# Product banks written whole before they are read, y a slot later, and token orders changed, in a fused GLA and S5 decoder block

## The chip, the cores and the metric

The kernel runs on one core of a Trainium2 chip. The metric is the device time of one execution in microseconds (us), and the time given is the median of several runs. Beside these runs stands one execution taken with the hardware profiler; from it come the profile's page and the answers of the trace. The engines are called as in the profile: PE is TensorE (PEld its weight loads), DVE is VectorE, ACT is ScalarE, POOL is GpSimd, SP is the engine that here only issues transfers. L60 means line 60 of the kernel.

## The reference, cut to what matters

One decoder block over 512 tokens of width 1024, all in fp32. 16 meta tokens stand ahead of the 512, so the mixers see 528 tokens.

```
h    = concat(meta, x);  xn = rmsnorm(h);  proj = xn @ w_in
q, k, v, r, a_low, u, z_gla, z_ssm = split(proj)
# GLA, 4 heads, key width 128, value width 256, chunks:
S_t  = diag(alpha_t) S_{t-1} + k_t^T v_t ;  o_t = q_t S_t      (alpha from a_low @ w_gate_up)
y_gla = (rmsnorm(o) * silu(r)) @ w_o_gla
# S5, 64 groups of 16 channels, 64 complex states each:
x_t  = Lbar x_{t-1} + Bbar u_t ;  y_t = Re(C x_t) + D u_t
y_ssm = glu(gelu(y) @ w_glu + b_glu)
mixed = sigmoid(z_gla) * y_gla + sigmoid(z_ssm) * y_ssm
h    = h + rmsnorm(mixed @ w_out)
f    = relu(rmsnorm(h) @ w_ff1)^2 @ w_ff2
out  = (h + rmsnorm(f)) without the meta tokens
```

## The kernel before, in words

**Products.** Every large product is made of three passes on PE. An fp32 operand is split into a rounded part and its remainder: ACT writes the rounded part (`split_hi`, L149), DVE subtracts it from the operand (L162 for weights, `wlo`). PE then adds hi x hi, hi x lo and lo x hi in one bank (`mm3`). A weight tile of 128 columns therefore costs a transfer of 512 KB on SP (`wraw`), one ACT and one DVE instruction, and 24 matmuls of 512 columns, or 48 of 264 columns where meta tokens are needed too. `xh` and `xl` hold the split, normalised input with features on the partitions and the 528 tokens along the columns, meta first.

**Banks.** There are two PSUM pools of four banks: `mm` for the large products, `sm` for small ones. A `sm` bank is taken again for the fifth allocation after it, once the readers of its old content are done. Two accesses of different engines to one bank are kept apart by a wait, also where they touch different halves.

**The mixer stage** is one long list, `dense`, of weight tiles. `slot()` takes the next tile, asks for the weights of the two tiles after it (`AHEAD = 2`, three buffers), and runs its matmuls and their epilogue. Between the slots stands the small work of the S5 scan (eight blocks of eight groups, class `Block`) and of the GLA heads (four, class `Head`; head h belongs to block h). In the order of one block b of the loop over blocks:

- `turns`: the rotation factors E of the block (DVE, ACT); then a slot
- `kernels`: turns MB into M1 on PE, makes the short kernel, issues the eight loads of U on SP; then `outputs` of the head before (products of scores and values and of queries and states, their squares on ACT, a chain of twelve small DVE steps to the row scale `ors`, and the scaled rows `on` on ACT) and `decays` of this head (exponentials from a load of `b2`); then a slot
- `scan`: M1 times U into `vv`, a swap of its halves by two transfers on POOL, rotation (L879), scan over chunks (L882), a second swap on POOL, rotation back (L885, L886), which gives X. On the side it stores the short kernel and issues the eight loads of M3. Then `turn_outputs` of the head before (transposes of `on`, one scaling, a store on POOL each); then a slot
- `turn_values`, a slot, `turn_keys`, a slot
- `scores` and `states` of this head. `states` makes four products, two to a bank; the first is copied out by DVE (L766), the others are added to the decayed state before (L769)
- `output`: y = M3 times U plus M2 times X in one bank, gelu on ACT and DVE, and eight stores on POOL (L903), which put y into phase order (token t of chunk c goes to column t*64 + c, with eight tokens to a chunk).

The order of PE's instructions through this stage is pinned to the order of the program. The order of the other engines' instructions, and of the transfers in each issuing queue, is set by a planner from its own estimates, before the kernel runs; at run time every queue is strictly in order.

**The merge** loads the eight tiles of gelu(y), splits them into `gh` and `gl` (L1008, L1009) while putting the tokens back into their order, and runs the GLU products; it reads the stored gates `zs` and GLA outputs `td`. Then come the output projection by tiles of 128 tokens (with a second load of x), and the feed-forward part, which is dense on PE to the end.

Of the kernel before, what the change touches and what calls it, by code (L numbers as in the profile page):

```python
# [22 lines left out]
HALF = NT // 2  # L23
# [13 lines left out]
T8 = 8  # L37
# [12 lines left out]
def hybrid_block(ctx: ExitStack, tc: tile.TileContext, io, out: bass.AP):  # L50
# [169 lines left out]
    xh, xl = (mk(px, [P, KT, LINE + SEQ], F32R, tag=t)[:, :, LINE - NM :] for t in ("xh", "xl"))  # L220
# [4 lines left out]

    def u_half(w, ut, q):
        ps = bank("mm")
        last = feat_tile(w, xh, xl, q * HALF, (q + 1) * HALF, ps[:, :HALF])
        S.copy(ut[:, :, q * 33 : (q + 1) * 33].rearrange("p s c -> p c s"), ps[:, :HALF].rearrange("p (c s) -> p c s", s=T8))
        return last  # L230
# [13 lines left out]
    xm = mk(pxt, [P, D], tag="xt", bufs=5)  # L244
    nc.scalar.dma_start(grow, io["g_mix_pre"][0].rearrange("(o d) -> o d", o=1))
    nc.scalar.dma_start(xm[:NM], io["meta_tokens"])
    xts = [(xm, NM, 0)]
    for t in range(TT):
        xt = mk(pxt, [P, D], tag="xt", bufs=5)
        loaded = nc.sync.dma_start(xt, io["x"][0, t * P : (t + 1) * P, :])  # L250
        xts.append((xt, P, NM + t * P))
# [13 lines left out]
    V.memset(ss[:, 0:1], 1.0)  # L265
    for i, (xt, n, col) in enumerate(xts):
        sq = mk(pxt, [P, D], tag="xsq", bufs=2)
        squared = S.activation(sq[:n], xt[:n], AF.Square, accum_out=ss[:n, i : i + 1])
        if i == 0:
            continue  # L270
        a = 0 if i == 1 else i
        root(rs[:, a : i + 1], ss[:, a : i + 1], pxt, f"xr{min(i, 2)}")
        for xt, n, col in xts[a : i + 1]:
            j = (col + P - 1) // P
            xn = mk(pxt, [P, D], tag="xn", bufs=2)
            normed = V.scalar_tensor_tensor(xn[:n], xt[:n], rs[:n, j : j + 1], gpre[:n], op0=ALU.mult, op1=ALU.mult)
            with ExitStack() as after:
                if i > 2:
                    after.enter_context(tc.issue_after(fed.ins))
                transpose_tokens(xn[:n], n, xh, xl, col)  # L280
        if i == 2:
# [3 lines left out]
        if i in (2, 3):  # L285
            fed = u_half(uw[i - 2], uts[i - 2], 0)
# [20 lines left out]
    for c in [0] + [NM + P * i for i in range(TT)]:  # L307
        G.memset(mask01[:, c : c + 1], 0.0)
# [10 lines left out]
    def low_rank():  # L319
        for i in range(2):  # L320
            sl = slice(i * HALF, (i + 1) * HALF)
            ps = bank("mm")
            for k in range(KT):
                PE.matmul(ps[:32, :HALF], wa[:, k, :], xh[:, k, sl], start=(k == 0), stop=False, skip_group_check=True)
                PE.matmul(ps[:16, :HALF], wa[:, k, :16], xl[:, k, sl], start=False, stop=(k == KT - 1), skip_group_check=True)
            S.copy(alow[:, sl], ps[:32, :HALF])
# [5 lines left out]
    def gate_up(h):  # L332
        for i in range(2):
            sl = slice(i * HALF, (i + 1) * HALF)
            ps = bank()
            PE.matmul(ps[:, :HALF], wgu[:, h * P : (h + 1) * P], alow[:, sl], start=True, stop=True)
            bg = vecs[:, V_BGATE + h : V_BGATE + h + 1]
            S.activation(ga[:, h, sl], ps[:, :HALF], AF.Abs, bias=bg)
            V.tensor_scalar(mn[:, h, sl], ps[:, :HALF], bg, 0.0, op0=ALU.add, op1=ALU.min)
# [316 lines left out]
    class Head:  # L656
# [10 lines left out]
        def value(self, w):  # L667
            vt = mk(pgb, [P, NT], tag="vt", bufs=2)
            for i in range(2):
                ps = bank("mm")  # L670
                feat_tile(w, xh, xl, i * HALF, (i + 1) * HALF, ps[:, :HALF])
                S.copy(vt[:, i * HALF : (i + 1) * HALF], ps[:, :HALF])
            self.vt.append(vt)

        def turn_values(self):
            self.vtok = mk(pgb, [P, TT, DV], tag="vtok", bufs=2)
            self.vmeta = mk(pgb, [NM, DV], tag="vmeta", bufs=2)
            for j, vt in enumerate(self.vt):
                cc = slice(j * P, (j + 1) * P)
                ps = bank()  # L680
                for t in range(TT):
                    PE.transpose(ps[:, t * P : (t + 1) * P], vt[:, NM + t * P : NM + (t + 1) * P], ident)
                S.copy(self.vtok[:, :, cc], ps.rearrange("p (t c) -> p t c", t=TT))
            ps = bank()
            for j, vt in enumerate(self.vt):
                PE.transpose(ps[:NM, j * P : (j + 1) * P], vt[:, :NM], ident)
            S.copy(self.vmeta, ps[:NM, :DV])

        def decays(self):
            b2 = mk(pgb, [P, NT], tag="b2")  # L690
            nc.sync.dma_start(b2, bd[self.h])
            bm = b2[:, NM:].rearrange("p (c t) -> p c t", t=CH)
            bp = b2[:, NM:].rearrange("p (c t) -> p c t", t=P)
# [7 lines left out]
            V.tensor_sub(dl[:, NM:].rearrange("p (c t) -> p c t", t=P), bp, bp[:, :, P - 1 : P].to_broadcast([P, TT, P]))  # L701
            V.tensor_scalar(dl[:, :NM], b2[:, :NM], b2[:, NM - 1 : NM], None, op0=ALU.subtract)
# [10 lines left out]
            self.qg = ex([P, SEQ], b2[:, NM:], "gq", 1.0 / TAU)  # L713

        def key(self, w):
            kT = mk(pgb, [P, NT], tag="kT")
            for i in range(2):
                ps = bank("mm")
                feat_tile(w, xh, xl, i * HALF, (i + 1) * HALF, ps[:, :HALF])
                S.copy(kT[:, i * HALF : (i + 1) * HALF], ps[:, :HALF])  # L720
            V.tensor_mul(self.kg, kT, self.kg)
            V.tensor_mul(self.kin, kT[:, NM:], self.kin)
            V.tensor_mul(self.kx, kT[:, NM:].rearrange("p (c t) -> p c t", t=P)[:, :, :CH], self.kx)

        def query(self, w):
            qs = DK ** -0.5
            ps = bank("mm")
            feat_tile(w, xh, xl, NM, NT, ps)
# [4 lines left out]
        def turn_keys(self):  # L733
            kg = self.kg
            ps = bank()
            for t in range(TT - 1):
                PE.transpose(ps[:, t * P : (t + 1) * P], kg[:, NM + t * P : NM + (t + 1) * P], ident)
            PE.transpose(ps[:NM, 3 * P : 4 * P], kg[:, :NM], ident)
# [18 lines left out]
        def states(self):  # L757
            self.st = []
            for t in range(TT):
# [445 lines left out]
```

## Time and profile before

| what | value |
|---|---|
| median of 3 runs | 1024.34 us (1023.4 to 1025.26) |
| the profiled execution | 1023.0 us, span 1021.3 us |
| PE busy | 963.2 us (94% of the span) |
| DVE, ACT, POOL busy | 559.1, 380.8, 92.8 us |
| mean granted clock of PE | 0.959 |
| a block of the mixer stage with a head | 59.0 us (207.69 to 266.72) |

The span is the profiled execution without what lies around it. A row of waits reads: the engine and its bank's name, then `<-` the engine, tile and line that released it, then microseconds in total, how many times, and the longest. A row of the timeline has start and duration in microseconds, then the engine, line, operation and tiles; square brackets hold the idle time before the first of the group and its releaser. A row of windows has the stretch, its length, and for each engine its busy time and number of instructions; then comes PE's granted clock (1.00 is full) and the transfers' share. A row of groups gives the busy time and the mean in nanoseconds of one instruction.

### The profile page before, as it was taken

To read this page: it belongs to the slowest core of one execution; us is meant where nothing else is said; L and a number is where in the kernel's file an instruction comes from. 1 tells how busy PE (TensorE), PEld (TensorE's weight loads), DVE (VectorE), ACT (ScalarE), POOL (GpSimd) and SP (SyncE) were. 2 spreads that over 40 slices of the span, in tenths; PEclk is the share of its full clock that TensorE was granted. 3 is DMA by queue.
4 is the path that set the end of the run, shared out by engine and by line. 5 is a ranking of instruction groups with operands and counts; after the bars stand their busy time and mean duration, and the time that the engine had idled before them with its cause. 6 is when DMAs were issued, how large, how long until landed. Compare 5 with 4: busy or idle time off the path is not lost.

```text
span 1021.3 us, 13307 instructions
## 1 busy us (share of the span) xinstructions
PE 963.2 (94%) x5052; PEld 824.0 (81%) x5052; DVE 559.1 (55%) x1003; ACT 380.8 (37%) x614; POOL 92.8 (9%) x189
## 2 busy tenths in 40 slices
PE   5999989989797999899989999999999999999997
PEld 4898969879696888788868887798888888888885
DVE  6779974645647469764445466563333343333335
ACT  6354534534443244222234244443232233233222
POOL 1220101111020112212200000000000000000000
PEclk9999988979698899799999999999999999999998
DMA  6835452425234266475585566123333354323302
GB/s 199 181 118 152 133 142 53 127 55 135 59 72 121 53 170 165 122 188 145 162 268 155 154 189 202 63 83 103 86 101 103 95 192 146 98 88 104 102 23 83
DMA packets 156801, 127.42 MB, mean 125 GB/s; under 512 B 22541, under 2 KB 137297, under 8 KB 156738
## 3 DMA queue, kind: packets, MB, share of 16 engines
q1 hardware_dynamic: 147472, 103.14, 36.2%
q0 software_dynamic: 8224, 20.74, 6.9%
q10 hardware_dynamic: 1042, 2.69, 0.7%
q8 instruction: 40, 0.66, 0.3%
q14 instruction: 23, 0.19, 0.1%
HBM read 103.37 MB, written 18.91 MB: 120 GB/s over the span
## 4 chain that ended last, share of the span: by engine, by line
PE 66%; issue 13%; DVE 10%; DMA 5%; ACT 3%; POOL 2%; DVEq 0%; POOLq 0%; SPq 0%; ACTq 0%
PE mm L60 47%; PE sm L60 18%; DMA vv<-vv 2%; DVE wlo L162 2%; DMA qi<-qd 1%; PE sm L65 1%; DMA wraw<-in_w_out_dram 1%; DVE vv L885 1%; ACT whi L149 1%; DMA wraw<-in_w_in_dram 1%; DMA wraw<-in_w_ff_dram 0%; DVE epb L210 0%; DVE ht L1089 0%; DVE mta L209 0%; DVE vv L886 0%
## 5 line engine op out<-in xcount | busy, mean ns | idle before, releaser
L162 DVE TENSOR_TENSOR wlo<-wraw,whi 128x1024 fp32r<-128x1024 f32 x104 | 126.9, 1220 | 150.3 <-ACT whi L149 143.8
L149 ACT ACTIVATE whi<-wraw 128x1024 fp32r<-128x1024 f32 x104 | 110.0, 1059 | 241.3 <-PE mm L60 223.9
L60 PE MATMUL mm<-xh,whi 128*128 128x264 f32 (+1 forms) x544 | 186.5, 343 | 0.3 <-ACT xh L149 0.3
L60 PE MATMUL mm<-xl,whi 128*128 128x264 f32 (+1 forms) x544 | 182.2, 335 | 0.7 <-DVE xl L187 0.7
L60 PE MATMUL mm<-xh,wlo 128*128 128x264 f32 (+1 forms) x544 | 181.7, 334 | 0.0
L60 PEld LDWEIGHTS mm<-xh,whi 128*128 128x128 f32 x544 | 106.6, 196 | 10.5 <-ACT xh L149 1.0
L60 PEld LDWEIGHTS mm<-xl,whi 128*128 128x128 f32 x544 | 106.4, 196 | 9.8 <-DVE xl L187 1.2
L60 PEld LDWEIGHTS mm<-xh,wlo 128*128 128x128 f32 x544 | 106.0, 195 | 9.2
L60 PE MATMUL mm<-hh,wlo 128*128 128x512 f32 (+1 forms) x280 | 103.9, 371 | 0.0
L60 PE MATMUL mm<-hl,whi 128*128 128x512 f32 (+1 forms) x280 | 103.8, 371 | 0.0
L60 PE MATMUL mm<-hh,whi 128*128 128x512 f32 (+1 forms) x280 | 103.8, 371 | 0.0
L1147 DVE TENSOR_TENSOR fl<-f,fh 128x512 fp32r<-128x512 f32 x32 | 22.2, 693 | 90.7 <-ACT fh L149 90.6
L149 ACT ACTIVATE fh<-f 128x512 fp32r<-128x512 f32 x32 | 20.2, 632 | 108.4 <-PE sm L60 104.7
L60 PEld LDWEIGHTS mm<-hh,whi 128*128 128x128 f32 x280 | 52.8, 188 | 9.1
L60 PEld LDWEIGHTS mm<-hh,wlo 128*128 128x128 f32 x280 | 52.8, 188 | 9.0
L60 PEld LDWEIGHTS mm<-hl,whi 128*128 128x128 f32 x280 | 52.8, 188 | 9.0
L60 PE MATMUL mm<-gh,whi 128*128 128x512 f32 x128 | 50.1, 396 | 3.2 <-ACT gh L149 3.2
L60 PE MATMUL mm<-gl,whi 128*128 128x512 f32 x128 | 50.5, 397 | 1.4 <-DVE gl L1009 1.4
L60 PE MATMUL mm<-gh,wlo 128*128 128x512 f32 x128 | 49.9, 395 | 0.0
L60 PE MATMUL sm<-U,M 128*128 128x65 f32 (+1 forms) x256 | 48.9, 315 | 0.0
L60 PEld LDWEIGHTS sm<-U,M 128*128 128x128 f32 x256 | 44.6, 235 | 1.4
L1143 DVE TENSOR_TENSOR w2l<-wraw,w2h 128x1024 fp32r<-128x1024 f32 x32 | 39.1, 1225 | 10.1 <-ACT w2h L149 10.1
(386 smaller groups left out, 1726.0 us busy)
## 6 DMA issues: line engine op xcount, KB each, us to landing
wraw<-in_w_ff_dram SPq DMA_DIRECT2D x64, 512.0 KB, 3.8
wraw<-in_w_in_dram SPq DMA_DIRECT2D x48, 512.0 KB, 4.3
wraw<-in_w_glu_dram SPq DMA_DIRECT2D x16, 512.0 KB, 4.2
vv<-vv POOLq DMA_DIRECT2D x32, 130.0 KB, 4.2
xt<-in_x_dram SPq DMA_DIRECT2D x8, 512.0 KB, 6.2
M<-kpad SPq DMA_DIRECT2D x64, 64.0 KB, 4.9
wraw<-in_w_o_gla_dram SPq DMA_DIRECT2D x8, 512.0 KB, 4.4
wraw<-in_w_out_dram SPq DMA_DIRECT2D x8, 512.0 KB, 4.3
```

What stands on the lines that cost most here:

```text
L60: ins = nc.tensor.matmul(*args, **kw)
L65: ins = nc.tensor.transpose(*args, **kw)
L149: S.activation(dst, src, AF.Copy, scale=scale)
L162: V.tensor_sub(lo[:, :, :n], raw[:, :, :n], f32(hi)[:, :, :n])
L885: V.tensor_mul(vv, vv, self.E)
L1143: V.tensor_sub(lo, raw, f32(hi))
L1147: V.tensor_sub(fl, f[:, k], f32(fh))
```

## The change

- **Whole banks.** `states` issues both products of a bank before DVE reads either; `outputs` issues all eight products of its two banks before ACT's squares.
- **Order of the blocks' small work.** `output` of block b moves behind `kernels` of block b+1; `outputs` of a head moves behind `scan`, with the exponential `qg` behind it (`query_decay`); `turn_outputs` moves behind `turn_values`. In blocks 6 and 7 one slot of five is left out; one more stands before the last `output`, and the list of tiles has three gates ahead of the r tiles instead of two.
- **Token order of S5.** The order of the columns after the merge stays the phase order of y. The sigmoid gates are written in that order (`by_phase`, `phases`: a read of the bank with a stride of eight columns), the GLA output's product reads its bank so, and the merge's splits become contiguous. Behind the output projection the rows of x and of the result are loaded and stored in pieces of 64 rows with a stride of eight tokens.
- **Meta tokens last.** The columns of `xh` and `xl` are the 512 tokens, then meta; halves of 256 and 272 columns take the place of two of 264. Meta is normalised after the four x tiles, each with a root of its own.
- The tiles `qi` of the merge get four buffers instead of two.

```diff
-HALF = NT // 2
+HALVES = ((0, 256), (256, NT))
...
-    xh, xl = (mk(px, [P, KT, LINE + SEQ], F32R, tag=t)[:, :, LINE - NM :] for t in ("xh", "xl"))
+    xh, xl = (mk(px, [P, KT, LINE + SEQ], F32R, tag=t)[:, :, :NT] for t in ("xh", "xl"))
...
     def u_half(w, ut, q):
+        a, b = HALVES[q]
         ps = bank("mm")
...
-        S.copy(ut[:, :, q * 33 : (q + 1) * 33].rearrange("p s c -> p c s"), ps[:, :HALF].rearrange("p (c s) -> p c s", s=T8))
+        src = ps.rearrange("p (c s) -> p s c", s=T8)
+        first = NM // T8 + a // T8
+        S.copy(ut[:, :, first : first + 32], src[:, :, :32])
+        if q:
+            S.copy(ut[:, :, : NM // T8], src[:, :, 32:34])
...
         squared = S.activation(sq[:n], xt[:n], AF.Square, accum_out=ss[:n, i : i + 1])
-        if i == 0:
-            continue
-        a = 0 if i == 1 else i
-        root(rs[:, a : i + 1], ss[:, a : i + 1], pxt, f"xr{min(i, 2)}")
...
+        root(rs[:n, i : i + 1], ss[:n, i : i + 1], pxt, "xr")
+        xn = mk(pxt, [P, D], tag="xn", bufs=2)
+        normed = V.scalar_tensor_tensor(xn[:n], xt[:n], rs[:n, i : i + 1], gpre[:n], op0=ALU.mult, op1=ALU.mult)
+        transpose_tokens(xn[:n], n, xh, xl, col)
...
+    def phases(t):
+        return t.rearrange("p (c t) -> p t c", t=T8)
+
+    def by_phase(t):
+        return t.rearrange("p (t c) -> p t c", t=T8)
+
     def gate_slot(c0, m, dst, tile_of):
         def go(w):
             ps = bank("mm")
-            feat_tile(w, xh, xl, NM, NT, ps)
+            feat_tile(w, xh, xl, 0, SEQ, ps)
             t = tile_of()
-            S.activation(t, ps, AF.Sigmoid)
+            S.activation(by_phase(t), phases(ps), AF.Sigmoid)
...
-            self.qg = ex([P, SEQ], b2[:, NM:], "gq", 1.0 / TAU)
+            self.b2, self.ex = b2, ex
+
+        def query_decay(self):
+            self.qg = self.ex([P, SEQ], self.b2[:, :SEQ], "gq", 1.0 / TAU)
...
-            for t in range(TT):
-                st = mk(pgb, [P, DV], tag="st", bufs=4)
...
+            for t in range(0, TT, 2):
+                pst = bank().rearrange("p (t v) -> p t v", t=2)
+                for i in range(t, t + 2):
+                    k, v = (self.ktok[:, i - 1, :], self.vtok[:, i - 1, :]) if i else (self.kmeta, self.vmeta)
+                    PE.matmul(pst[:, i % 2], k, v, start=True, stop=True)
+                for i in range(t, t + 2):
+                    st = mk(pgb, [P, DV], tag="st", bufs=4)
+                    if i == 0:
+                        V.tensor_copy(st, pst[:, 0])
+                    else:
+                        V.scalar_tensor_tensor(st, self.st[-1], self.dec[:, i - 1 : i], pst[:, i % 2], op0=ALU.mult, op1=ALU.add)
+                    self.st.append(st)
...
-            ops = []
+            ops = [bank().rearrange("p (t v) -> p t v", t=2) for _ in range(2)]
             for t in range(TT):
...
                 PE.matmul(po, self.qg[:, t * P : (t + 1) * P], self.st[t], start=False, stop=True)
+            for t in range(TT):
                 osq = mk(pgb, [P, DV], tag="osq", bufs=1)
-                S.activation(osq, po, AF.Square, accum_out=oss[:, t : t + 1])
+                S.activation(osq, ops[t // 2][:, t % 2], AF.Square, accum_out=oss[:, t : t + 1])
...
-            V.tensor_mul(zt, zt, ps)
+            V.tensor_mul(by_phase(zt), by_phase(zt), phases(ps))
...
         blk.kernels()
-        if before:
-            before.outputs()
-        if head:
-            head.decays()
+        if b:
+            blocks[b - 1].output()
+        if this:
+            this.decays()
         slot()
         blk.scan()
-        if before:
-            before.turn_outputs()
+        if last:
+            last.outputs()
+        if this:
+            this.query_decay()
+        next(following, None)
+        slot()
+        if this:
+            this.turn_values()
+        if last:
+            last.turn_outputs()
...
+        if b < 6:
+            slot()
+        if this:
+            this.scores()
+            this.states()
         next(following, None)
-        blk.output()
+    slot()
+    blocks[-1].output()
...
-        q = mk(pgl, [P, SEQ], tag="qi", bufs=2)
+        q = mk(pgl, [P, SEQ], tag="qi", bufs=4)
         nc.sync.dma_start(q, qd[m])
-        qp = q.rearrange("p (t c) -> p t c", t=T8)
-        ghp, glp = (t[:, m].rearrange("p (c t) -> p t c", t=T8) for t in (gh, gl))
-        split_hi(ghp, qp)
-        V.tensor_sub(glp, qp, f32(ghp))
+        split_hi(gh[:, m], q)
+        V.tensor_sub(gl[:, m], q, f32(gh)[:, m])
...
-        nc.sync.dma_start(xt, io["x"][0, ts_, :])
+        for i in range(2):
+            nc.sync.dma_start(xt[i * CH : (i + 1) * CH], io["x"][0].rearrange("(c t) d -> t c d", t=T8)[2 * t + i])
...
-            (nc.sync, nc.scalar)[n].dma_start(out[0, ts_, ns], ag[:, ns])
+            for i in range(2):
+                (nc.sync, nc.scalar)[n].dma_start(out[0].rearrange("(c t) d -> t c d", t=T8)[2 * t + i, :, ns], ag[i * CH : (i + 1) * CH, ns])
```

More of the change, by code (lines that the diff above doesn't have):

```diff
@@ L950, in hybrid_block @@
         following = blocks[b + 1].tables() if b + 1 < NBLK else iter(())
[L951 to L952 removed]
+        this = heads[b] if b < HEADS else None
+        last = heads[b - 1] if 0 < b <= HEADS else None
         blk.turns()
```

128 lines of the change are left out of this document (48 added, 80 removed).

## The prediction

> **What bounds the kernel now.** I read the page first, then the waits of TensorE (PE), then the granted clock in windows.
>
> ```profile
> span 1021.3 us, 13307 instructions
> PE 963.2 (94%) x5052; PEld 824.0 (81%) x5052; DVE 559.1 (55%) x1003; ACT 380.8 (37%) x614; POOL 92.8 (9%) x189
> PEclk9999988979698899799999999999999999999998
> ```
>
> PE is busy for 94% of the span, no other engine for more than 55%. So the time is PE's work, plus PE's idle time, plus what the work loses where the clock is not full. The clock row has its dips in slices 6 to 17, the mixer stage. PE's waits say who causes them:
>
> ```profile
> PE sm L60 <- DVE st L766: 19.3, 4, 5.2
> PE sm L60 <- ACT osq L783: 4.8, 8, 0.6
> PE sm L60 <- ACT whi L149: 4.5, 1, 4.5
> PE mm L60 <- ACT gh L149: 3.2, 3, 1.9
> PE sm L60 <- DVE st L769: 2.3, 4, 0.6
> PE mm L60 <- DVE gl L1009: 1.4, 3, 0.6
> PE sm L60 <- DVE vv L886: 1.2, 2, 1.0
> ```
>
> The largest wait comes four times, once per head, and each time is about 5 us. Here is one of them in order of time:
>
> ```profile
> 201.85 0.69 PE L60 MATMUL sm<-vmeta,kmeta 16*128 16x256 f32 x2
> 204.88 1.22 DVE L162 TENSOR_TENSOR wlo<-wraw,whi 128x1024 fp32r<-128x1024 f32 x1
> ...
> 207.21 0.42 DVE L766 COPY st<-sm 128x256 f32<-128x256 f32 x1
> 207.69 2.08 PE L60 MATMUL sm<-vtok,ktok 128*128 128x256 f32 x4 [5.15 <-DVE st L766]
> ```
>
> PE puts the first state product into one half of a bank, and the product for the other half starts only when VectorE (DVE) has copied the first half out. DVE gets to that copy late, because a split of weights and other work stand ahead of it. The price is more than the wait. Windows from the restart of PE to the clock's return (columns: length, PE busy, granted clock):
>
> ```profile
> 147.87:162.64 14.77, 14.20 (x58) 0.50 0.23 53
> 207.69:220.64 12.95, 12.37 (x50) 0.50 0.19 47
> 266.72:282.08 15.36, 14.78 (x61) 0.50 0.18 44
> 326.65:340.06 13.41, 12.84 (x45) 0.50 0.20 47
> 416.69:424.72 8.03, 8.03 (x34) 0.50 0.35 107
> 534.66:538.08 3.42, 3.42 (x10) 0.50 0.27 77
> ```
>
> After each such wait the clock is half for 13 to 15 us. The fifth window follows the one 4.5 us wait in block 5, the sixth the waits for gh and gl at the start of the merge.
>
> **The change, part by part.** The sum is made against the profiled run: 1023.0 us, of which 1021.3 is span; the median of the runs shown is 1.3 us above it, and I add that at the end.
>
> *States and outputs written whole, then read.* Both products of a bank go out back to back; only the reads wait. That removes the waits for st, 19.3 + 2.3, and for osq, 4.8: **26.4 us**. With no 5 us hole before them, the four half-clock stretches go too: (14.20 + 12.37 + 14.78 + 12.84) / 2 = **27.1 us**. What is late next? DVE's copies are no earlier, so the next bank they hold is asked for by the M1 transposes of the next block, behind a whole slot, which takes 5.80 us (below). The four state pairs last about 2.6 us (4 x 0.65, from 0.69 for the first), so PE would ask from about 201.85 + 2.6 + 5.80 + 0.5 = 210.8 on; the scores' bank was read before the copy of st began, at 207.2. That leaves 3.6 us, so I cost the shift at nothing here; without that cover the wait returns.
>
> [...]
>
> *y one slot further on.* In block 5 the products of y stopped for X, which was held by a DMA of the scan:
>
> ```profile
> 414.08 1.24 DVE L885 TENSOR_TENSOR vv<-vv,E 128x1040 f32<-128x1040 f32 x1 [3.09 <-DMA vv<-vv]
> ...
> 416.69 0.66 PE L60 MATMUL sm<-vv,M 128*128 128x64 f32 x2 [4.48 <-ACT whi L149]
> ```
>
> The named releaser, a split of weights, feeds no product of y; X comes out of DVE two instructions after the start of the first row, and that is what PE waited for. A slot and the M1 products now lie in between: 4.48 + 8.03 / 2 = **8.5 us** go, and the 1.2 us for vv L886.
>
> *Merge.* The splits of q, which wrote a stride of eight, become contiguous, and four loads are in flight instead of two:
>
> ```profile
> L1009 DVE TENSOR_TENSOR gl<-qi,gh 128x512 fp32r<-128x512 f32 x8 | 9.2, 1166 | 12.5 <-ACT gh L149 12.5
> L149 ACT ACTIVATE gh<-qi 128x512 fp32r<-128x512 f32 x8 | 9.2, 1174 | 12.8 <-DMA qi<-qd 12.8
> L1147 DVE TENSOR_TENSOR fl<-f,fh 128x512 fp32r<-128x512 f32 x32 | 22.2, 693 | 90.7 <-ACT fh L149 90.6
> L149 ACT ACTIVATE fh<-f 128x512 fp32r<-128x512 f32 x32 | 20.2, 632 | 108.4 <-PE sm L60 104.7 <-DVE f L1111 3.7
> L229 ACT COPY ut<-mm 128x264 f32<-128x264 f32 x16 | 10.3, 644 | 16.8 <-PE mm L60 10.5 <-issue 6.3
> L672 ACT COPY vt<-mm 128x264 f32<-128x264 f32 x16 | 5.9, 372 | 9.7 <-PE mm L60 9.7
> ```
>
> Contiguous splits of the same size take 632 and 693 ns instead of 1174 and 1166. At stake is the wait of 3.2 + 1.4 and half of 3.42: 6.3 us at most, nothing if the loads themselves are the limit. Since both halves of the chain (load, split) get shorter I take **4.5**.
>
> *Strided reads of a PSUM bank* come in for that: 16 gate sigmoids, 16 copies of u, 8 products in the output slots. The trace has none. Lower end: as contiguous. Upper end: as the strided writes, +0.54 on ACT and +0.48 on DVE per 512 columns. I take the middle of the two, since each moves the same elements: 16 x 0.27 = 4.3 us of ACT, 8 x 0.24 = 1.9 of DVE. All of it is behind PE's slots on engines that are 37% and 55% busy: nothing on the path. If it were on the path whole, at the upper end, it would be 16 x 0.54 + 8 x 0.48 = 12.5 us. The u copies lose their strided write (644 against 372 ns) and pay the read instead, plus eight copies of two columns; u is loaded blocks later.
>
> [...]
>
> *Order of the start.* Meta's normalisation no longer stands before that of the first x tile:
>
> ```profile
> 12.03 2.47 DVE L276 SCALAR_TENSOR_TENSOR xn<-xt,xrs,gpre 16x1024 f32<-16x1024 f32 x2
> ```
>
> Half of that, 1.2 us, comes off the first chain; an extra root and meta's transposes come later, ahead of u's second halves. Between -1 and +2.5 us; I take **1.0**. The halves 256 and 272 have the same 528 columns as 264 and 264: nothing.
>
> *Stores and loads by phase.* Four more loads of x on SP, hidden by the output projection, and 8 more stores, four each on SP and ACT; the last adds one issue to the end:
>
> ```profile
> 1018.25 0.34 ACTq L1178 DMA_DIRECT2D out_dram<-ag  x1
> ```
>
> **-0.4 us**, between 0 (half the bytes each) and -0.7.
>
> *What moves, and the new waits.* The outputs of a head go behind the scan, their turning behind that of the values, and y with its eight q stores comes ahead of the scan's stores on POOL.
>
> ```profile
> L903 POOL DMA_DIRECT2D qd<-q x64: 528/528/553, 162.6 to 503.6; - x64
> 232.49 0.59 PE L60 MATMUL sm<-st,e_gq 128*128 128x256 f32 x2
> 233.09 5.80 PE mm L60 x48
> 233.69 0.17 DVE L784 TENSOR_SCALAR oss<-oss 128x4 f32<-128x4 f32 x1 [1.32 <-ACT osq L783]
> 236.99 1.57 ACT L789 ACTIVATE on<-sm,ors 128x256 f32<-128x256 f32 x4 [0.58 <-DVE ors L146]
> 239.00 1.75 PE sm L60 x16
> 240.57 1.04 PE L65 MATMUL sm<-ident,on 128*128 128x128 f32 x8
> 247.22 1.26 PE L65 MATMUL sm<-ident,vt 128*128 128x128 f32 x10
> 247.32 1.24 DVE L879 TENSOR_TENSOR vv<-vv,E 128x1040 f32<-128x1040 f32 x1 [6.21 <-DMA vv<-vv]
> ```
>
> Today `on` is done 5.5 us after the outputs' end (233.08 to 238.56) and is asked for after 7.5. Then it is asked for after a slot and the turning of the values, 5.80 + 1.26 = 7.1 us: 1.6 to spare. But the small DVE steps that make `on` now share their time with the scan's, and the first of these, L879, waits for its DMA until 6.6 us after the scan's last product (240.75 to 247.32). DVE's queue is in order: whatever stands behind L879 waits too. The outputs are eight products of at most 0.60 us (232.49 to 233.09); since the next starts before the last has drained I take 3.4 us in all, so L879 starts 3.2 us after their end. It takes 1.24 us, the addition of half its columns about 0.7, the scan about 1.24 again: 3.2. If the whole chain of `on` (3.3 us on DVE from 233.69, 1.57 on ACT) stands behind, `on` comes at 3.2 + 3.2 + 3.3 + 1.57 = 11.3, that is 4.2 us late. If it stands ahead, nothing. The chain began 0.6 us after the outputs, so part of it gets through: I take 1.5 us for each of four heads, **-6 us**. For other banks asked for sooner by a faster PE I take **-2**, between 0 and -4.8 (the osq waits come back elsewhere). The eight q stores occupy POOL for 8 x 0.528 = 4.2 us; in blocks 1 to 7 the scan's stores can come that much later, still three slots ahead of their user: nothing, until they hold up DVE (below). U and M3 on SP are asked for no sooner relative to their users.
>
> **Sum:** 26.4 + 27.1 + 8.5 + 1.2 + 4.5 + 1.0 - 0.4 - 6 - 2 = 60.3 us off. 1023.0 - 60.3 = 962.7 for a profiled run, **964 us** by the median.
>
> **Rivals.** (1) *`on` is late enough to stop the clock.* For it: L879's 6.21 us hold. Against: 1.6 us of slack. At the full 4.2 us, four times, each with a half-clock stretch worth 6.8 (27.1 / 4), it costs 44 instead of 6: 964 + 38 = **1002**.
>
> (2) *The change doesn't do what it says; the st wait moves to the next bank.* For it: DVE is no earlier, and PE comes sooner. Against: 3.6 us of cover, and DVE's load:
>
> ```profile
> 207.69:266.72 59.03, 52.12 (x336) 47.13 (x336) 34.52 (x65) 26.52 (x51) 8.66 (x17) 0.88 0.37 91
> ```
>
> DVE has 34.5 us of work in a block of 59; at 46 us a block it is 75% busy. If waits and clock stay, only osq, y, merge and start remain: 4.8 + 8.5 + 1.2 + 4.5 + 1.0 - 0.4 = 19.6, giving 1024.3 - 19.6 = **1005**.
>
> (3) *Slower: POOL holds the scan.* If q comes late from ACT and DVE, its stores stand in POOL ahead of the vv stores, L879 waits longer, and all splits of weights stand behind it. Weights are fetched two slots ahead, so this decides once L879 is held for more than 2 x 5.80 = 11.6 us, against 6.21 today. Then PE stops for about 5 us in each of seven blocks and loses the clock: 7 x (5 + 6.8) = 83 us, against 68.3 won: **1039**. Against it: y ends a slot ahead of the scan, and POOL is busy for only 8.66 us of a block.
>
> **How the numbers follow.** The forecast has 0.64, with a range of its own of 946 to 982 from the bounds of the terms; still less time 0.04; rival 1 0.14; rival 2 0.11; rival 3 0.05; gains that cancel to no change 0.02. The halves of rivals 1 and 2 below 1002 bring the range to 946 to 1002. A difference under 0.2% could not be told from none; so faster 0.93, same 0.02, slower 0.05.
>
> **What would show it.** Right: no PE wait for st or osq, a granted clock of 1.00 from 140 us to the merge, blocks of about 46 us instead of 59, no wait at y, gh and gl at about 0.63 and 0.69 us. Wrong: a PE wait on `on` at the turning of the outputs, on sc or st at the M1 transposes, on a wlo behind a held L879, or a half-clock stretch after any of them.

## The result and the profile after

The changed kernel takes **993.37 us** (median of 4 runs, 990.22 to 996.54); the kernel before took 1024.8 us in the same job. The ratio is 0.9682, with a 95% interval of [0.9626, 0.9738]: faster by 3.2%. The forecast was 964 us, with a range of 946 to 1002. The time is inside the range, and about half of the forecast gain is missing. The bounds of the forecast's own terms, 946 to 982 us, do not hold it; the range reached up to 1002 only to allow for rivals 1 and 2, and neither of them came. That the time lies inside is in so far luck.

The page of the changed kernel, profiled at 995.96 us:

```profile
span 994.3 us, 13327 instructions
PE 950.2 (96%) x5052; PEld 818.2 (82%) x5052; DVE 554.8 (56%) x1008; ACT 371.4 (37%) x623; POOL 93.1 (9%) x189
PEclk9999998999998997887999999999999999999998
```

Of the dips in slices 6 to 14 two shallow ones are left (slices 7 and 13), and there is a new run of them in slices 16 to 19, late in the mixer stage. PE's waits in the changed kernel, in the columns used before, without those of the start:

```profile
PE sm L60 <- DVE vv L891: 16.1, 3, 7.5
...
PE sm L65 <- ACT vtok L686: 3.1, 3, 1.0
...
PE sm L60 <- DMA zi<-zgd: 1.9, 1, 1.9
...
PE mm L60 <- DVE gl L1018: 0.6, 1, 0.6
```

No wait for `st` or `osq` is left. In their place PE waits three times for `vv` L891, the last step of X, which y reads. The 1.9 us put down to `zi` stand ahead of the first product of y in block 6. The windows of the changed kernel's mixer stage in which the clock was half (length, busy time with the number of instructions for PE, PEld, DVE, ACT and POOL, granted clock, transfers):

```profile
153.80:160.80 7.00, 7.00 (x35) 7.00 (x35) 3.25 (x6) 3.12 (x5) 0.00 (x0) 0.51 0.35 82
297.20:304.00 6.80, 6.80 (x28) 6.22 (x28) 3.08 (x5) 1.23 (x2) 0.00 (x0) 0.50 0.40 96
375.60:389.40 13.80, 10.88 (x41) 9.92 (x42) 12.67 (x24) 3.13 (x5) 0.19 (x1) 0.51 0.13 35
416.60:430.40 13.80, 9.95 (x39) 9.23 (x40) 7.39 (x16) 1.55 (x3) 0.26 (x1) 0.51 0.20 59
457.60:471.40 13.80, 10.77 (x41) 9.89 (x42) 3.32 (x4) 1.23 (x2) 1.11 (x3) 0.51 0.15 49
```

The last three stand around the three waits and cost, by an estimate of half of PE's busy time in them, (10.88 + 9.95 + 10.77) / 2 = 15.8 us. The first two are of another kind: PE has no idle time in them or ahead of them. By the same estimate they cost (7.00 + 6.80) / 2 = 6.9 us.

Where the time went, by the first instruction of each stage (the transposes of `kt` open a block's scan; `gh` opens the merge, `hh` the feed-forward part):

| stretch | before, us | after, us | difference |
|---|---|---|---|
| start to the scan of block 0 | 121.8 | 120.0 | -1.8 |
| scans of blocks 0 to 3 | 177.0 | 138.6 | -38.4 |
| scan of block 3 to the merge | 219.8 | 237.7 | **+17.9** |
| merge to the output projection | 94.9 | 88.0 | -6.9 |
| output projection to the first `hh` | 49.6 | 49.3 | -0.3 |
| first `hh` to the end | 358.2 | 360.7 | +2.5 |

The sum is -27.0 us, as the spans say. The first half of the mixer stage did what was forecast; the second half became slower than before.

**Why X comes late.** The chain that PE waits for at the y of block 6, from the changed kernel's timeline of POOL, then of DVE, then of PE:

```profile
389.21 4.23 POOL L908 DMA_DIRECT2D qd<-q  x8 [16.73 <-DVE q L906]
...
395.50 0.54 POOL L878 DMA_DIRECT2D vv<-vv  x1
...
401.09 1.23 DVE L162 TENSOR_TENSOR wlo<-wraw,whi 128x1024 fp32r<-128x1024 f32 x1 [0.23 <-ACT whi L149]
406.53 1.23 DVE L162 TENSOR_TENSOR wlo<-wraw,whi 128x1024 fp32r<-128x1024 f32 x1 [4.21 <-ACT whi L149]
407.67 1.24 DVE L884 TENSOR_TENSOR vv<-vv,E 128x1040 f32<-128x1040 f32 x1
...
411.05 0.69 DVE L931 TENSOR_TENSOR zi<-zi,mm 128x512 f32<-128x512 f32 x1 [1.41 <-PE mm L60]
411.66 1.24 DVE L887 TENSOR_TENSOR_SCAN vv<-d,vv 128x520 f32<-128x520 f32 x1
...
418.42 1.24 DVE L890 TENSOR_TENSOR vv<-vv,E 128x1040 f32<-128x1040 f32 x1 [4.41 <-DMA vv<-vv]
419.69 0.70 DVE L891 TENSOR_TENSOR vv<-vv 128x520 f32<-128x520 f32 x1
...
420.45 0.69 PE L60 MATMUL sm<-vv,M 128*128 128x64 f32 x2 [4.61 <-DVE vv L891]
```

L884, the first rotation, stands in DVE's queue behind a split of weights that itself waited 4.21 us for PE, although the queue's work before that was done at 402.3, and the swap that it needs, issued on POOL behind the eight stores of q, had landed at 400.8. The planner has put it there. L887, the scan, stands behind a product L931 that waits for PE's next slot. So the first rotation and the scan are each tied to a slot of PE, and y, which comes four slots behind its scan (three in blocks 6 and 7), stops for X: for 4.61 us here, for 7.5 us in block 7.

**Merge, reads of banks, tail.** Groups of the changed kernel:

```profile
L149 ACT ACTIVATE gh<-qi 128x512 fp32r<-128x512 f32 x8 | 4.9, 626 | 4.5 <-DMA qi<-qd 4.5
L1018 DVE TENSOR_TENSOR gl<-qi,gh 128x512 fp32r<-128x512 f32 x8 | 5.4, 690 | 3.5 <-ACT gh L149 3.5
L387 ACT ACTIVATE ut<-mm 128x512 f32<-128x512 f32 x11 | 6.5, 590 | 0.1
L931 DVE TENSOR_TENSOR zi<-zi,mm 128x512 f32<-128x512 f32 x8 | 5.5, 688 | 17.6 <-PE mm L60 17.6
```

The contiguous splits take 626 and 690 ns, as forecast. The last two read a bank with a stride of eight; the kernel before did the same work on contiguous columns:

```profile
L384 ACT ACTIVATE ut<-mm 128x512 f32<-128x512 f32 x10 | 5.9, 593 | 0.1
L926 DVE TENSOR_TENSOR zi<-zi,mm 128x512 f32<-128x512 f32 x8 | 5.5, 684 | 14.7 <-PE mm L60 14.6
```

593 against 590 ns and 684 against 688: the strided read of a bank costs nothing here, while the strided write to SBUF of the old splits took 1.7 to 1.9 times as long (1166 and 1174 ns against 690 and 626). The tail of the changed kernel, in the chain that ended last and in ACT's timeline:

```profile
972.46 0.54 ACTq L1189
973.03 0.84 ACTq L1189
973.98 0.70 ACT junk L1060 x2
...
989.66 1.35 ACTq L1189 DMA_DIRECT2D out_dram<-ag  x2
```

A token tile's two store issues in a row take 1.35 us of ACT where one took 0.34, and the squares of the next tile wait behind them. The products of PE from the first `hh` on take 350.9 us in both kernels; what grew is the time behind the last of them, from 7.4 to 9.8 us. How much of that is the squares' wait is measured below ("The last stores off ACT").

### The profile page after: what moved, and what is told of

The parts are those of the page before. It is cut to its first block, busy times and chain, and to the rows that moved or that the text cites. A ratio compares the mean times of both kernels' runs of the same rounds, so it can differ in the third digit from the quotient of the medians.

```text
span 994.3 us, 13327 instructions
## 1 busy us (share of the span) xinstructions
PE 950.2 (96%) x5052; PEld 818.2 (82%) x5052; DVE 554.8 (56%) x1008; ACT 371.4 (37%) x623; POOL 93.1 (9%) x189
## 4 chain that ended last, share of the span: by engine, by line
PE 72%; DVE 8%; issue 8%; DMA 4%; ACT 3%; POOL 3%; ACTq 0%; DVEq 0%; POOLq 0%; SPq 0%
PE mm L60 55%; PE sm L60 15%; DMA vv<-vv 2%; PE sm L65 2%; POOL qd L908 2%; DMA wraw<-in_w_out_dram 1%; DMA qi<-qd 1%; DVE vv L890 1%; ACT junk L1060 0%; DMA wraw<-in_w_ff_dram 0%; DVE wlo L162 0%; ACT on L794 0%; DVE ht L1099 0%; ACTq L1189 0%; ACT L700 0%
## 5 line engine op out<-in xcount | busy, mean ns | idle before, releaser
L60 PE MATMUL mm<-xh,whi 128*128 128x512 f32 (+2 forms) x544 | 186.6, 343 | 1.3 <-ACT xh L149 0.8
L60 PE MATMUL mm<-xl,whi 128*128 128x512 f32 (+2 forms) x544 | 181.9, 334 | 1.6 <-DVE xl L187 1.6
L60 PE MATMUL mm<-xh,wlo 128*128 128x512 f32 (+2 forms) x544 | 182.0, 334 | 0.0
L60 PE MATMUL sm<-vv,M 128*128 128x64 f32 x128 | 33.1, 351 | 16.1 <-DVE vv L891 16.1
L908 POOL DMA_DIRECT2D qd<-q x64 | 33.8, 536 | 128.0 <-DVE q L906 125.1
```

The source lines that it names most:

```text
L60: ins = nc.tensor.matmul(*args, **kw)
L908: nc.gpsimd.dma_start(qd[self.blk].rearrange("(g h) (t c) -> t h g c", h=HG, t=T8)[t], q[t * HG : (t + 1) * HG].rearrange("h (g c) -> h g ...
```

## The experiments

The theory after the result (**Y**): writing the banks whole is worth what was forecast, and the new place of y is what loses it again, by waits for X and by half clock. It has three parts. A: the stores of q stand ahead of the scan's on POOL. B: blocks 6 and 7 lack a slot between scan and y. C: y right behind the small products of `kernels` makes the clock fall without any idle time. The rival (**R**): the strided reads, or a head's outputs behind the scan, cost it by the load on ACT and DVE. The diffs are against the changed kernel unless another is named.

**Only the banks, on the kernel before.** The `states` and `outputs` of the change, and nothing else of it.

```
 (kernel before)
+            for t in range(0, TT, 2):            # states: two products, then two reads
+                pst = bank().rearrange("p (t v) -> p t v", t=2)
...
+            ops = [bank().rearrange("p (t v) -> p t v", t=2) for _ in range(2)]   # outputs
```

> The kernel before, with only the states and outputs written whole before they are read; everything else (y at the end of its block, meta first, token order) as before. If the prediction's first two terms are right, PE's waits for st and osq (26.4 us) and the four half-clock stretches behind them (27.1 us) go, blocks with a head last about 47 us, and the time is 1024.8 - 53.5 = 971, with the 4.5 us wait at y in block 5 still there. Rival: the other moves are needed to use the time (DVE is no earlier, PE waits at the next bank or at y instead): 1000 or more.

971.44 us (970.09 to 973.9), ratio 0.9488 [0.9464, 0.9513]. That is 53.7 us off 1025.14; the terms of the prediction for the waits and the clock behind them were 26.4 + 27.1 = 53.5. So the whole remainder of the change made the kernel slower, by 22 us.

**The stores of q behind the scan's** (part A).

```
+            self.q = q
+
+        def store(self):
+            q = self.q
             for t in range(T8):
                 nc.gpsimd.dma_start(qd[self.blk]...
...
         blk.scan()
+        if b:
+            blocks[b - 1].store()
```

> The changed kernel, with the eight stores of q put behind the stores of the scan of the same block on POOL; y's products stay where the change put them. Theory A (the q stores and what waits for them stand ahead of the scan's stores, and the scan's DVE work is planned late for it): the waits for vv L891 (16.1 us) and the half-clock stretches behind them (15.6 us) go for the most part, 993 - 25 = 968. Theory B (blocks 6 and 7 have a slot too few between scan and y): the waits stay, 988 to 993.

984.91 us (983.49 to 987.97), ratio 0.9621 [0.9594, 0.9648]: 8.5 us faster, a third of what A expected. PE's waits and, for one head, DVE's timeline of this run:

```profile
PE sm L65 <- ACT on L794: 10.7, 7, 2.8
PE sm L60 <- DVE vv L891: 0.5, 1, 0.5
...
222.37 1.24 DVE L884 TENSOR_TENSOR vv<-vv,E 128x1040 f32<-128x1040 f32 x1 [5.72 <-DMA vv<-vv]
...
224.27 0.16 DVE L789 TENSOR_SCALAR oss<-oss 128x4 f32<-128x4 f32 x1
```

A holds for the waits: those at y fall from 16.1 to 0.5 us. But the planner now puts L884 ahead of the chain that makes `on` (its first step is L789). L884 waits 5.72 us for its swap, the chain stands behind it, and PE waits 10.7 us for `on`. In the changed kernel the same chain runs at 220.07, ahead of L884 at 227.56:

```profile
220.07 0.17 DVE L789 TENSOR_SCALAR oss<-oss 128x4 f32<-128x4 f32 x1 [5.23 <-ACT osq L788]
227.56 1.24 DVE L884 TENSOR_TENSOR vv<-vv,E 128x1040 f32<-128x1040 f32 x1
```

So whoever is late on DVE changes places: in the one order `on` is late, in the other X is. Beside that there are four falls of the clock without idle time (6.8 us each, from 202.2, 256.8, 389.9 and 424.1), which cost 13.7 us, where the changed kernel had two that cost 6.9. The waits for `on` and these falls take back most of what A expected.

**Five slots kept in blocks 6 and 7** (part B).

```
-        if b < 6:
-            slot()
+        slot()
```

> The changed kernel, with the fifth slot kept in blocks 6 and 7 (the one that the change leaves out there). Theory B: the two waits of 7.5 us at y of blocks 6 and 7 shrink by a slot of 5.4 us each, to 2 us, and the half-clock stretches behind them (10.2 us) go: 993 - 20 = 973; the wait of 4.0 in block 5 stays. Theory A: the waits shrink by less than half, since the scan's DVE work stays behind the splits, 985 to 993.

985.07 us (981.8 to 985.57), ratio 0.9612 [0.9586, 0.9637], at the fast edge of what A expected and 12 us over B's number. The slot does take its part of the waits, 16.1 to 4.9 us over two blocks (the expectation took the waits in blocks 6 and 7 for 7.5 us each; the changed kernel's trace has 4.61 and 7.49):

```profile
PE sm L60 <- DVE vv L891: 4.9, 2, 3.4
```

The clock does not follow: in this run's windows there are three falls without idle time (from 153.4, 204.6 and 300.1), where the changed kernel had two, and two of 13.8 and 10.4 us around the remaining waits.

**y behind the scan and the outputs of the next block**, still later and away from the small products.

```
         blk.kernels()
-        if b:
-            blocks[b - 1].output()
...
             this.query_decay()
+        if b:
+            blocks[b - 1].output()
```

> The changed kernel, with y one slot further still: behind scan and outputs of the next block, so that the scan's stores come ahead of the q stores, and y no longer follows the M1 transposes and kernel products. Theories A and B both: no wait at y in blocks 5 and 6, 993 - 20 = 973, the wait in block 7 (whose y stands where it stood) may stay. Theory C (the half-clock stretches of 7.6 and 6.4 us in blocks 1 and 4, with no idle time before them, come from y standing right behind the narrow products): these two go as well, another -7, 966. If C is wrong they appear behind y at its new place.

992.39 us (992.09 to 994.71), ratio 0.9696 [0.9669, 0.9724]: no gain, a miss of some 20 us. The waits at y are gone; PE's largest in this run is another:

```profile
PE sm L65 <- ACT on L794: 18.5, 4, 6.8
```

The gelu of y now shares ACT and DVE with the scan and with the chain of `on`, and `on` pays again, more than with q's stores late. It is the exchange of places once more. C's part of the expectation came: with y away from the small products of `kernels`, each fall of the clock in this run has idle time ahead of it.

**y back at the end of its own block, five slots in every block**; all the rest of the change stays.

```
         blk.kernels()
-        if b:
-            blocks[b - 1].output()
...
-        if b < 6:
-            slot()
+        slot()
...
         next(following, None)
-    slot()
-    blocks[-1].output()
+        blk.output()
```

> The changed kernel with y back at the end of its own block and five slots in every block; all the rest of the change stays. Theory Y: the new place of y (with the slot left out in blocks 6 and 7) is the whole of what the change lost against the run with only the banks written whole (971.4 us); the rest of the change is worth -6.9 (merge), -2.3 (start), +2.5 (tail) and about +3 (waits for vtok), so 965 to 969 us, no half-clock stretch without idle time before it, and one wait of about 4 us at y in block 5 as before. Rival R: the strided reads and the heads' outputs behind the scan cost as well, by the load on ACT and DVE: 975 us or more, with waits at vtok, on or the splits of weights.

969.69 us (965.0 to 971.74), ratio 0.9437 [0.9393, 0.9481]: 23.7 us faster than the changed kernel. Y expected 965 to 969, R 975 or more; the time is 0.7 us above Y's range. No half clock without idle time ahead of it is left. At the y of blocks 5 to 7 waits remain (1.12, 2.79 and 1.25 us), each with a fall behind it, where one wait of about 4 us was expected.

**Only the move of y**, on the kernel with only the banks.

```
 (kernel with only the banks written whole)
         blk.kernels()
+        if b:
+            blocks[b - 1].output()
...
-        slot()
+        if b < 6:
+            slot()
...
-        blk.output()
+    slot()
+    blocks[-1].output()
```

> The run with only the banks written whole (971.4 us) plus the new place of y and the slot left out in blocks 6 and 7, nothing else of the change. Theory Y: it takes on what the changed kernel shows there: 16.1 us of waits at y, 15.6 of half clock behind them, 7.2 of half clock without idle time, less the 3.8 and about 5 that y costs in block 5 in its old place: 971.4 + 30 = 1001 us (994 to 1006). Rival R: the cost comes from the other parts, and the move alone stays within 5 us of 971.4 or gains.

990.87 us (989.33 to 993.41), ratio 0.9652 [0.9614, 0.969]: 19.4 us lost by the move alone, without token order, strided reads or later outputs. The sign is Y's, and R's 5 us are passed; the size is two thirds of the 30 expected. The wait is there again (13.2 us, up to 7.8), and so is a fall without idle time (from 200.4).

**The heads' outputs where they were**, on the run with y back.

```
 (run with y back)
+        if last:
+            last.outputs()
         if this:
             this.decays()
+            this.query_decay()
         slot()
         blk.scan()
...
```

> As e5, and the outputs of a head ahead of the scan again, their turning right behind it and the values a slot later, all as in the kernel before; token order of the S5 output, meta last and four loads in the merge stay. Theory Y: the waits for vtok (3.1 us) go, nothing comes: 962 to 966, within 5 us of e5. Rival R, in so far as the place of the outputs is what costs: 8 us or more below e5.

967.9 us (965.91 to 971.04), ratio 0.9436 [0.9392, 0.9481]. Against 0.9437 with the outputs behind the scan there is no difference. With y in its old place, where the outputs stand doesn't matter; R falls.

**The last stores off ACT**, on the run with y back.

```
 (run with y back)
-                (nc.sync, nc.scalar)[n].dma_start(out...
+                (nc.sync, nc.scalar if t == TT - 1 else nc.sync)[i].dma_start(out...
```

> As e5, with all last stores of the first three token tiles on SP's queue and those of the last tile one each on SP's and ACT's per half, so that ACT never has two stores back to back. Theory: two issues back to back hold ACT for 1.35 us in place of 0.34 and delay the next squares; without that the tail (first product with hh to the end) falls from 360.7 to about 358.2, and the time is 2.5 us under e5 (1.5 to 3). Rival: the tail is longer for the smaller pieces, not for the issues: within 1 us of e5.

**962.39 us** (956.15 to 963.8), ratio 0.9361 [0.9315, 0.9406]: faster than both kernels, 31 us under the changed one. All four executions lie under all four of the run with y back. Only a part of the 7.3 us between the two is the tail: from the first `hh` to the end it takes 359.6 us against 360.6, so 1.0 of the 2.5 expected came. The squares of the last tile now follow PE's last product at once, but the last tile's two stores on ACT still fall together (1.39 us). That the remaining 1.3 us over the kernel before come from these two issues and not from the smaller pieces is not shown. What is left of the difference lies ahead of the merge, where both kernels have the same instructions in the same order on every engine. There the profiled runs differ in the clock, by some 5 us, and in the waits at y, by some 1 us; this pair is taken up at the end.

**A sixth slot ahead of y in blocks 5 to 7**, on the last kernel.

```
 (run with the last stores off ACT)
+        if b > 4:
+            slot()
         blk.output()
```

> As e8, with a sixth slot ahead of y in blocks 5, 6 and 7, taken from the ten slots that stood behind the last y; the work is the same. Theory Y (what y lacks is time between its own scan and itself, 5.8 us at most): the 4.3 us of waits at y in these blocks go, and the half clock behind them (5.1 us in e8's profile, up to 10 in e5's): 950 to 957 us, against 962.4 for e8. Rival: the last stores of y come so late that the merge waits for them; then a wait for gh of 5 us or more comes back, and the time is 960 or more.

965.86 us (963.99 to 967.77), ratio 0.9403 [0.9375, 0.943]: the rival's number. PE's waits:

```profile
PE mm L60 <- ACT gh L149: 10.8, 1, 10.8
PE sm L60 <- DVE vv L891: 0.8, 1, 0.8
```

Y's half is right: with one more slot the waits at y fall from 4.3 to 0.8 us and no clock falls ahead of the merge; PE is through with the mixer stage at 455.8 (466.6 less the wait), 7.9 us before the kernel without the sixth slot. But the expectation counted ten slots behind the last y; the trace shows four, of which this run leaves one. The loads of q for the merge are issued right behind the last store of q (458.48 against 458.27 us), its first split waits for them, and the 7.9 us are given back.

**The small products of `kernels` twice**, on the run with y back (the same values written again).

```
 (run with y back)
-                for g in range(4):
+                for g in 2 * list(range(4)):
                     PE.transpose(... self.MB[:, g0 + g] ...
-            for g in range(GB):
+            for g in 2 * list(range(GB)):
                 PE.matmul(... self.M2 ... BA ...
```

> As e5, with the products of the kernels (eight transposes of MB, eight products of 16 columns) issued twice into the same bank, so that TensorE has 5.2 us of small products in a row, as the changed kernel has with y behind them, but nothing of y there. The extra work itself is 8 x 2.6 = 21 us. Theory C (a long run of small products makes the clock fall with no idle time before it): half-clock stretches of 6 to 9 us right behind these products in two blocks or more, each losing 3 to 4.5 us, so 969.7 + 21 + 7 or more = 997 us or more. Rival (the fall in the changed kernel came from something in y, such as its wait for X): no such stretch, 969.7 + 21 = 991 us (987 to 994).

1000.63 us (1000.41 to 1002.55), ratio 0.9746 [0.9716, 0.9776], past the 997 that C asked for and 6 us over the rival's upper end. The small products of one block (from 207 us on), and the windows of half clock in two:

```profile
206.77 1.25 PE L65 MATMUL sm<-ident,MB 128*128 128x128 f32 x10
207.86 3.64 PE L60 MATMUL sm<-BA,M 128*128 128x16 f32 x32
...
212.60:216.00 3.40, 3.40 (x18) 3.40 (x17) 2.64 (x4) 0.12 (x1) 0.00 (x0) 0.50 0.00 1
264.00:267.20 3.20, 3.20 (x17) 3.20 (x17) 3.06 (x5) 0.04 (x1) 0.00 (x0) 0.50 0.31 78
```

In seven of the eight blocks the clock falls behind the doubled products, with PE busy throughout and no y near. The stretches are shorter than expected, 3.4 us each, so by the estimate of half they cost 7 x 1.7 = 12 us; the rest, 19 of 31 us, is about the added work, which had been put at 21.

## Why the prediction was half right

**Whole banks: right.** 53.5 us were forecast for the waits and the clock behind them, and the run with only the banks gave 53.7. The reading that 3.6 us cover what is late next holds: no wait moved to the next bank (rival 2).

**y one slot further on: wrong, and this is the step that failed.** The prediction booked 8.5 + 1.2 = 9.7 us as won, by counting the slot that the move adds between scan and y. What it overlooked is on the other side: when X is ready. It says of the scan's stores that they "can come that much later, still three slots ahead of their user: nothing, until they hold up DVE (below)", and costs that condition only as rival 3. The 4.2 us on POOL were right. But in the planner's new order the scan's DVE steps stand behind splits and products that wait for PE's next slot: in block 6 L884 starts 6.9 us after its swap has landed. With q's stores moved behind the scan's, that order and the waits at y are gone. In blocks 6 and 7 the list also gives the added slot back; the prediction has no term for it, and keeping that slot took 11.2 us of the waits away. Instead of 9.7 us less, y costs 16.1 us of waits, 15.8 of half clock around them and 6.9 of half clock without a wait, 38.8 in all (without the 1.9 us put down to `zi` ahead of the y of block 6). Putting y back returns 23.7 us of it, since y costs something in the old place too; moving y alone costs 19.4.

Rival 3 named this mechanism (POOL holds the scan, q's stores ahead) and gave it a chance of 0.05, with the victim wrong: it looked for PE stopping on splits behind a held first rotation (L879 before, L884 after). What stopped was y itself.

**A second omission: the clock also fell with PE busy.** The prediction took idle time for the only cause. The 6.9 us, with PE busy through both windows, and the seven falls of 3.4 us with the doubled products show falls without it. It also read the 13 to 15 us of half clock as what one stop of 5 us costs. The rows of the last section show y's products of 64 columns at half clock for 6.4 us right behind a stop; that they kept the clock down so long is the author's reading, which no run tried. The 27.1 us came out right: in the run with only the banks, without the stops, the clock reads 1.00 from 100 to 360 us.

The other terms, against the stage table and the waits:

| term | forecast, us off | measured, us off |
|---|---|---|
| whole banks, waits and clock | 53.5 | 53.7 |
| y | 9.7 | 9.7 - 38.8 = -29.1 |
| merge | 4.5 | 6.9 |
| start | 1.0 | 1.8 |
| last stores | -0.4 | -2.5 |
| new waits of the heads (`on`) | -6 | -3.1 (`vtok`) |
| other banks | -2 | 0 |
| sum | 60.3 | 27.7 (the profiled times give 27.0) |

*Merge:* the direction and the sizes of the splits (0.63 and 0.69 forecast, 0.626 and 0.690 measured) were right. The gain passes the bound of 6.3 by a little; that bound came from the waits and the half clock alone. *Strided reads:* middle price 0.27 and 0.24 us more per instruction; measured none. They were booked as hidden, so the sum did not feel it. *Last stores:* the upper end, -0.7, counted one issue more at the end. It left out that the issues of the first three tiles hold ACT ahead of the next squares, and that the second issue in a row takes longer than the first (0.84 to 0.86 us against 0.47 to 0.54). *`on`:* no wait in the changed kernel, since there its chain runs ahead of L884. The run with q's stores late has the mechanism of the prediction: L884 held, the chain behind it, 10.7 us for four heads, 2.7 each and thus between the ends of 0 and 4.2 that it gave.

The list of signs at the end of the prediction worked: no `st`, no `osq`, gh and gl at their sizes, blocks 1 and 2 at 47.0 us instead of 59; and the sign that failed, "no wait at y", led to the cause.

## What to carry to other kernels

A consumer that is moved later is safe only against the producer as it will then run: follow the producer's chain through each queue that the same edit loads, and look which of its steps come to stand behind an instruction that waits for the engine you want to free (here L884, behind a split that itself waited 4.21 us). Time one part of a bundled change alone before believing the bundle: here one edit of two loops was worth 54 us, and the rest of the change took 22 us of it back. And short products were no free filler for PE here: behind 3.41 us of products of 16 and 64 columns, and 0.41 us of transposes among them at most, the clock was half for 6.83 us in two blocks of five, without a wait.

## What the runs showed of the hardware

**The falls read here lie on one grid of 3.41 us.** Read to a hundredth, the five half-clock windows of the changed kernel's mixer stage begin at 153.83, 297.19, 375.70, 416.66 and 457.62 us. The distances are 143.36, 78.51, 40.96 and 40.96: 42, 23, 12 and 12 steps of 3.413 us. Their lengths (6.83 and 13.65) are 2 and 4 such steps; the short ones with the doubled products (3.4) and the shortest of the kernel before (3.41) are 1. The pair with one instruction order has a fall and none at one place: the same y of block 5 with nearly the same wait, in the run with y back (first two rows) and in the run with the last stores off ACT.

```profile
359.50 0.41 PE L60 MATMUL sm<-vv,M 128*128 128x64 f32 x2 [1.12 <-DVE vv L891]
361.39 0.64 PE L60 MATMUL sm<-vv,M 128*128 128x64 f32 x2
...
359.19 0.41 PE L60 MATMUL sm<-vv,M 128*128 128x64 f32 x2 [1.15 <-DVE vv L891]
361.44 0.39 PE L60 MATMUL sm<-vv,M 128*128 128x64 f32 x2
```

In the first the products slow from 0.39 to 0.64 us at 361.2, in the second they do not, after a wait that is 0.03 us longer. In the first, one step of the grid (357.8 to 361.2) holds the wait and 1.9 us of y; in the second a step ends at 359.7 (11 steps before its one fall at 397.2) and parts them. That the place on the grid decides whether a wait or a run of small products costs a fall is the author's reading of this pair. In their profiles the first kernel falls at the y of blocks 5, 6 and 7, for 20.6 us in all, the second at one of them, for 10.4; by the estimate of half, 5.1 us, that is most of the 7.3 us between them. Why the second was luckier in all of its runs is not settled.

**The clock fell behind products of 16 columns.** In the first five blocks of the changed kernel y stands behind the small products of `kernels`, and PE does not wait for X. Here are the steps of the grid with the most of y in them, all at full clock and with PE busy throughout; PE's time is that of the 16-column products alone, the rest being y's products of 64 columns (and 0.41 us of transposes in the fourth):

```profile
150.42:153.83 3.41, 1.66 (x15) 1.00 0.17 37
201.62:205.03 3.41, 0.63 (x6) 1.00 0.40 118
249.40:252.81 3.41, 0.00 (x0) 1.00 0.47 123
293.78:297.19 3.41, 1.86 (x16) 1.00 0.25 86
338.15:341.56 3.41, 0.71 (x7) 1.00 0.00 0
```

Behind the first and the fourth step the clock falls, to 0.50 for 6.83 us each; behind the others it does not, though the third holds nothing but products of 64 columns. So the same instructions cost a fall in two blocks and none in three; the steps ahead of the two falls hold 1.66 and 1.86 us of the 16 columns, the other three 0.71 at most. With the doubled products the clock falls in seven blocks; around those of the eighth (block 1, its `kt` at 168.4 us) it reads 1.00 from 124 to 212 us. How much of each form goes with a fall was not measured.

**In the falls read here full clock came 2.4 to 6.2 us after the first large product.** This is the y of block 6 in the changed kernel, from its last product on; it had begun at 420.45, behind the wait of 4.61 us:

```profile
426.48 0.64 PE L60 MATMUL sm<-vv,M 128*128 128x64 f32 x2
426.87 0.77 PE L60 MATMUL mm<-ogh,whi 128*128 128x512 f32 x1
...
430.38 0.40 PE L60 MATMUL mm<-ogh,wlo 128*128 128x512 f32 x1
```

For 6.4 us after the stop PE makes nothing but y's products of 64 columns, all at half clock. The first large product starts at 426.87, and from 430.3 on the clock is full, 3.4 us later. In the five falls of the changed kernel's mixer stage full clock comes 2.8 to 4.4 us after the first large product, and behind the four long stops of the kernel before, where the state products and y come first, 2.6 to 5.0 us; behind its wait in block 5 it is 2.4. The longest case is the run with a sixth slot: 6.2 us, with 0.6 us of idle time in the step in which the products begin. So the 13.8 us of half clock are the rest of the stop, y's products at half clock, and at most 4.4 us of large products.

**A second store issue in a row on ACT's queue** took 0.84 to 0.86 us in the changed kernel, behind a first of 0.47 to 0.54, against 0.34 to 0.35 for one alone in the kernel before.
